# Fewer candidates and four queues: the expert selection of a diffusion backbone on one core

## The chip, the cores and the metric

The kernel runs on one core of a Trainium2 chip. The metric is the device time of one execution in microseconds. The engines are TensorE (PE; its weight loads are PEld), VectorE (DVE), ScalarE (ACT), GpSimd (POOL) and SyncE (SP), which here only issues transfers. TensorE's clock is granted at 2.4 or 1.2 GHz; the profile gives the granted share.

## What is computed

A backbone of two layers over 512 latent tokens and, in layer 0, 256 context tokens. Each layer has a mixer and then a block (PEER) that picks experts for each token. Only that block is touched by the change. Of it, for each block of 128 tokens:

```python
q = (xb @ w_q).reshape(PEER_BLOCK, PEER_HEADS, 2, PEER_DHALF)
s = jnp.einsum('thpd,hpkd->thpk', q, subkeys).astype(jnp.float32)
s1, i1 = lax.top_k(s[:, :, 0], PEER_TOPK)
s2, i2 = lax.top_k(s[:, :, 1], PEER_TOPK)
cand = (s1[..., :, None] + s2[..., None, :]).reshape(PEER_BLOCK, PEER_HEADS, PEER_TOPK * PEER_TOPK)
cidx = (i1[..., :, None] * PEER_NKEYS + i2[..., None, :]).reshape(PEER_BLOCK, PEER_HEADS, PEER_TOPK * PEER_TOPK)
top, pos = lax.top_k(cand, PEER_TOPK)
idx = jnp.take_along_axis(cidx, pos, axis=-1)
g = jax.nn.softmax(top, axis=-1)
ue, ve = u[idx], v[idx]
act = jax.nn.gelu(jnp.einsum('td,thkd->thk', xb, ue).astype(jnp.float32), approximate=False)
return jnp.einsum('thk,thkd->td', (g * act).astype(xb.dtype), ve)
```

There are 8 heads, 128 keys in each half, 16 picks and a model width of 1024; the tables `u` and `v` have 16384 rows in each layer.

## The kernel before

The layers run one after the other: the mixer, then `peer_u`, then `peer_v0` or `peer_v1`. Every fp32 product is made of three matmuls of a high and a low half; ScalarE writes the high half (`uh`, `wqh`, `pqh`, `vh`) and VectorE, sometimes GpSimd, the low half (`ul`, `wql`, `pql`, `vl`) by a subtraction (`split`, L106 and L109).

`peer_u` treats the tiles of 128 tokens in two ways. For the first `ng` tiles (two in layer 0, one in layer 1) it gathers the picked rows of `u` (L899, GpSimd) and takes a dot product with the token on VectorE (L905). For the other `n - ng` tiles (four, three) TensorE multiplies the whole table with the tokens, in 128 steps of 128 table rows (`proj`, L674); ScalarE takes the Gelu (`ga`, L991) and the result goes to DRAM. The gates of these tiles are spread to all 16384 rows by matmuls of one-hot rows (`prep` makes `p1`, `p2e` and `p2` on VectorE, L834 to L837; `gbuild` multiplies, L851, and ScalarE copies to `stg`), and are stored in `gd`. The next stage, `peer_v0` or `peer_v1`, loads them (`gf`) and multiplies them in (L1037).

The first sixteen steps also have a projection each (`q_items`): `project` (the queries of one half of a head), `evac` (`pqh`, `pql`, L717 and L718), `score` (the products with the keys, whose matmuls read `pql`) and `top`, a search of the 16 largest of 128 scores for each tile (`topk16`: five finding instructions, L643 to L647). The weights' low halves `wql` come from GpSimd but for the first two, all `skl` too (`q_load`).

The picks are side work (`stage2`). `cands` adds all 256 pairs of the two lists of 16 for two heads (L766) and searches the 16 largest of 256; `decode` turns a position into the two key numbers by comparing it with 0 to 15 and summing (L789 to L794); `rows` makes the row numbers for the gathers; `soft` is the softmax over a tile's heads (Exp on ScalarE, L802).

What sets the order: at the end of each step a loop takes pieces from three queues (the gathered tiles with their dots in one, the gates of the others, and the modulation products of `mod_items`) by the largest share that is left, until the costs written beside the pieces have used up what the step gives; a piece is held to stand behind `ul` of the next step (`issue_after`). Each engine then works in the order in which its instructions stand. `ul` and `uh` have a raised priority. The searches of the step are issued ahead of this loop:

```python
if 1 <= c <= 2 * PH:
    for f in qi[c - 1][3]:
        f()
```

Of the kernel before, what the change touches and what calls it, by code (L numbers as in the profile page):

```python
# [21 lines left out]
P = 128  # L22
# [3 lines left out]
NLAT = 512  # L26
# [45 lines left out]
def kernel(ctx: ExitStack, tc: tile.TileContext, a: dict, out: bass.AP, dbg=None, stop=None):  # L72
# [13 lines left out]
    tok = [a["tok"][t * P:(t + 1) * P, :] for t in range(NT)]  # L86

# [561 lines left out]
    def peer_u(layer, tiles):  # L649
# [4 lines left out]
        gd = dram.tile([TD // 32, P, P, 32], F32, name=f"gd{layer}")  # L654
# [3 lines left out]
        with ExitStack() as s1:  # L658
# [9 lines left out]
            def proj(ps, wh, wl, blks):  # L668
                for k in range(KD):
                    for x, q in ((wh, 0), (wh, 1), (wl, 0)):  # L670
# [9 lines left out]
                      allow_small_or_imprecise_dtypes=True)  # L680
            urow = [up.tile([P, P], U32, name=f"urow{j}", bufs=1) for j in range(ng)]
# [6 lines left out]
            def q_load(hp):  # L688
# [4 lines left out]
                split(wh, wl, w, eng_lo=vec if hp < 2 else pool)  # L693
# [4 lines left out]
                split(skh, skl, sk, eng_lo=pool)  # L698
# [42 lines left out]
            side, pend, stores = [], [], []  # L741

            def store():
                b, stg, j = stores.pop(0)
                js = slice(j, j + P // GS)
                nc.scalar.dma_start(gd[b][:, js], stg[:, js])
# [5 lines left out]
            def stage2(t):  # L752
                d = {}

                def alloc():
                    d["top"] = up.tile([P, PH, TOPK], F32, name="top", bufs=3)
                    d["pos"] = up.tile([P, PH, TOPK], U32, name="pos", bufs=3)
                    d["if"] = up.tile([P, 16, TOPK], F16, name="if16", bufs=3)
                    d["id"] = [up.tile([P, PH, TOPK], F32, name=f"id{q}", bufs=3) for q in range(2)]

                def cands(h0):
                    def f():
                        vv = v16[t].rearrange("p (h q) k -> p h q k", q=2)
                        c = up.tile([P, 2, TOPK, TOPK], F32, name="cand", bufs=1)
                        hs = slice(h0, h0 + 2)
                        vec.tensor_tensor(c, vv[:, hs, 0, :, None].to_broadcast([P, 2, TOPK, TOPK]),  # L766
                                          vv[:, hs, 1, None, :].to_broadcast([P, 2, TOPK, TOPK]), op=ALU.add)
                        for h in range(2):
                            w_ = up.tile([P, 256], F32, name="candw", bufs=1)
                            topk16(d["top"][:, h0 + h, :], d["pos"][:, h0 + h, :],  # L770
                                   c[:, h].rearrange("p x y -> p (x y)"), w_)
                    return f

                def decode(h0):
                    def f():
                        iv = d["if"].rearrange("p (h q) k -> p h q k", q=2)
                        hs = slice(h0, h0 + 2)
                        qs = slice(2 * h0, 2 * h0 + 4)
                        vec.tensor_copy(d["if"][:, qs], i16[t][:, qs])
                        for q in range(2):  # L780
                            pi = up.tile([P, 2, TOPK], U32, name="pi")
                            if q == 0:
                                vec.tensor_scalar(pi, d["pos"][:, hs], 4, None, op0=ALU.logical_shift_right)
                            else:
                                vec.tensor_scalar(pi, d["pos"][:, hs], 15, None, op0=ALU.bitwise_and)
                            pf = up.tile([P, 2, TOPK], F16, name="pif")
                            vec.tensor_copy(pf, pi)
                            eq = up.tile([P, 2, TOPK, TOPK], F16, name="eq", bufs=1)
                            vec.tensor_tensor(eq, pf[:, :, :, None].to_broadcast([P, 2, TOPK, TOPK]),  # L789
                                              i16v[:, None, None, :].to_broadcast([P, 2, TOPK, TOPK]),  # L790
                                              op=ALU.is_equal)
                            vec.tensor_tensor(eq, eq, iv[:, hs, q, None, :].to_broadcast([P, 2, TOPK, TOPK]),
                                              op=ALU.mult)
                            vec.tensor_reduce(d["id"][q][:, hs], eq, axis=AX.X, op=ALU.add)  # L794
                    return f

                def soft():
                    top = d["top"]
                    g = up.tile([P, PH, TOPK], F32, name="g")
                    sm = up.tile([P, PH], F32, name="gsm")  # L800
                    vec.tensor_tensor(g, top, top[:, :, 0:1].to_broadcast([P, PH, TOPK]), op=ALU.subtract)
                    act.activation(g, g, AF.Exp)  # L802
                    vec.tensor_reduce(sm, g, axis=AX.X, op=ALU.add)
                    vec.reciprocal(sm, sm)
                    vec.tensor_tensor(g, g, sm[:, :, None].to_broadcast([P, PH, TOPK]), op=ALU.mult)
                    d["g"] = g
# [74 lines left out]
                for h0 in range(0, PH, 2):  # L881
                    out_ += [(cands(h0), 4.9), (decode(h0), 3.8)]
# [755 lines left out]
```

## Time and profile before

| | |
|---|---|
| Median of 3 runs | 4072.78 us (4063.73 to 4077.03) |
| The profiled execution | 4070.86 us |
| Its span | 4069.1 us |
| TensorE busy | 3779.4 us, 93% |
| TensorE weight loads | 3221.3 us, 79% |
| VectorE busy | 3287.3 us, 81% |
| ScalarE busy | 1463.4 us, 36% |
| GpSimd busy | 1394.4 us, 34% |
| Transfers | 1036.47 MB, 255 GB/s on average |

Busy times are unions over the whole span; TensorE's matmuls overlap each other, so its share is no measure of distance from its peak. The stages follow each other: layer 0's `peer_u` from 475 to 1632 us, `peer_v0` to 2345, layer 1's mixer to 2726, its `peer_u` to 3516, `peer_v1` to the end.

### The profile page before, as it was taken

To read this page: it belongs to the slowest core of one execution; us is meant where nothing else is said; L and a number is where in the kernel's file an instruction comes from. 1 tells how busy PE (TensorE), PEld (TensorE's weight loads), DVE (VectorE), ACT (ScalarE), POOL (GpSimd) and SP (SyncE) were. 2 spreads that over 40 slices of the span, in tenths; PEclk is the share of its full clock that TensorE was granted. 3 is DMA by queue.
4 is the path that set the end of the run, shared out by engine and by line. 5 is a ranking of instruction groups with operands and counts; after the bars stand their busy time and mean duration, and the time that the engine had idled before them with its cause. 6 is when DMAs were issued, how large, how long until landed. Compare 5 with 4: busy or idle time off the path is not lost. (4 is left out here: it accounts for less than half of the span.)

```text
span 4069.1 us, 53545 instructions
## 1 busy us (share of the span) xinstructions
PE 3779.4 (93%) x19201; PEld 3221.3 (79%) x19201; DVE 3287.3 (81%) x6594; ACT 1463.4 (36%) x2384; POOL 1394.4 (34%) x1010
## 2 busy tenths in 40 slices
PE   6988989999999897999999989888999999899998
PEld 5766777877777675788888789867899999788887
DVE  7776698998999897888888864458898987588887
ACT  4354422233232333322232355542234344333333
POOL 2521225303423244666666412215302222132221
PEclk9999989999999998999999999988999999999999
DMA  7301446548979799999999721046448779799995
GB/s 245 100 3 52 172 141 240 177 167 301 342 261 356 274 368 363 387 390 390 387 391 389 283 84 46 18 172 220 164 159 319 266 268 331 286 385 363 356 356 216
DMA packets 409099, 1036.47 MB, mean 255 GB/s; under 512 B 33024, under 2 KB 167680, under 8 KB 408832
## 3 DMA queue, kind: packets, MB, share of 16 engines
q1 hardware_dynamic: 259360, 498.68, 35.3%
q0 software_dynamic: 114336, 416.34, 27.9%
q10 hardware_dynamic: 35136, 118.05, 7.5%
q8 instruction: 150, 2.46, 0.2%
q14 instruction: 117, 0.96, 0.1%
HBM read 906.05 MB, written 126.88 MB: 254 GB/s over the span
## 5 line engine op out<-in xcount | busy, mean ns | idle before, releaser
L899 POOL DMA_INDIRECT urows<-in_u_rows,urow x384 | 487.5, 1270 | 1124.1 <-DVE urows L905 639.4
L1048 POOL DMA_INDIRECT vrows<-in_v_t,vrow x384 | 594.2, 1547 | 592.5 <-DVE accg L1056 340.1
L674 PE MATMUL aps<-pnh,uh 128*128 128x512 f32 (+1 forms) x2048 | 770.0, 376 | 22.0 <-ACT ga L991 18.4
L674 PE MATMUL aps<-pnh,ul 128*128 128x512 f32 (+1 forms) x2048 | 763.6, 373 | 26.3 <-DVE ul L109 26.0
L674 PE MATMUL aps<-pnl,uh 128*128 128x512 f32 (+1 forms) x2048 | 759.6, 371 | 0.0
L106 ACT CAST uh<-uf 128x1024 fp32r<-128x1024 f32 x256 | 269.2, 1051 | 839.2 <-PE aps L674 815.9
L905 DVE SCALAR_TENSOR_TENSOR urows<-urows,px 128x1024 f32<-128x1024 f32 x384 | 468.7, 1231 | 66.1 <-DMA urows<-in_u_rows,urow 65.4
L106 ACT CAST vh<-vf 128x1024 fp32r<-128x1024 f32 x256 | 269.3, 1053 | 594.5 <-DMA vf<-in_v_t 279.9
L674 PEld LDWEIGHTS aps<-pnh,ul 128*128 128x128 f32 x2048 | 389.8, 190 | 78.7 <-DVE ul L109 34.2
L674 PEld LDWEIGHTS aps<-pnh,uh 128*128 128x128 f32 x2048 | 391.5, 191 | 72.0 <-ACT ga L991 25.4
L109 DVE TENSOR_TENSOR vl<-vf,vh 128x1024 fp32r<-128x1024 f32 x256 | 312.6, 1221 | 166.0 <-ACT vh L106 155.9
L674 PEld LDWEIGHTS aps<-pnl,uh 128*128 128x128 f32 x2048 | 390.5, 191 | 43.2
L109 DVE TENSOR_TENSOR ul<-uf,uh 128x1024 fp32r<-128x1024 f32 x256 | 320.2, 1251 | 79.5 <-ACT uh L106 70.3
L1079 PE MATMUL acc<-vh,vwh 128*128 128x512 f32 x1024 | 317.7, 392 | 23.9 <-ACT vwh L106 23.8
L1079 PE MATMUL acc<-vh,vwl 128*128 128x512 f32 x1024 | 317.3, 391 | 1.3 <-DVE vwl L109 1.1
L1079 PE MATMUL acc<-vl,vwh 128*128 128x512 f32 x1024 | 317.5, 391 | 0.0
L1056 DVE SCALAR_TENSOR_TENSOR vacc<-vrows,gw,vacc 128x1024 f32<-128x1024 f32 x254 | 313.8, 1277 | 0.0
L851 PE MATMUL gps<-p,p 128*128 128x128 f16 x1792 | 243.9, 296 | 14.1 <-DVE p L837 14.1
L1144 PE MATMUL acc<-vh,vwh 128*128 128x512 f32 x768 | 239.3, 393 | 15.2 <-ACT vwh L106 12.1
L1079 PEld LDWEIGHTS acc<-vh,vwh 128*128 128x128 f32 x1024 | 192.8, 189 | 66.2 <-ACT vwh L106 26.4
L851 PEld LDWEIGHTS <-p 128*128 128x128 f16 x1792 | 189.1, 118 | 62.7 <-issue 38.6
L1144 PE MATMUL acc<-vl,vwh 128*128 128x512 f32 x768 | 238.2, 392 | 0.0
(430 smaller groups left out, 7540.8 us busy)
## 6 DMA issues: line engine op xcount, KB each, us to landing
uf<-in_u_t SPq DMA_DIRECT2D x256, 512.0 KB
vf<-in_v_t SPq DMA_DIRECT2D x256, 512.0 KB
gd<-stg ACTq DMA_DIRECT2D x112, 512.0 KB
wmt<-in_w_modT SPq DMA_DIRECT2D x90, 512.0 KB
gad<-ga ACTq DMA_DIRECT2D x64, 512.0 KB
gaf<-gad SPq DMA_DIRECT2D x64, 512.0 KB
gf<-gd SPq DMA_DIRECT2D x32, 1024.0 KB
gad<-ga ACTq DMA_DIRECT2D x64, 384.0 KB
```

The lines of the kernel that those rows point to most:

```text
L106: act.copy(hi, src)
L109: return el.tensor_tensor(lo, src, hi.bitcast(F32), op=ALU.subtract)
L674: pe.matmul(ps[:, o:o + w], x[:, k, :], blk[q][:, k, :w], start=(k == 0 and x is wh and q == 0), stop=(k == KD - 1 and x is wl))
L851: pe.matmul(gp[:, i * P:(i + 1) * P], p1[:, g, :, i], p2[q][:, g, :, i], start=q == 0, stop=q == 1)
L899: nc.gpsimd.indirect_dma_start(out=r, out_offset=None, in_=a["u_rows"], in_offset=bass.IndirectOffsetOnAxis(ap=urow[j][:, k:k + 1], axis=0))
L905: vec.scalar_tensor_tensor(r, r, 1.0, PK["x"][j], op0=ALU.mult, op1=ALU.mult, accum_out=gact[j][:, k:k + 1])
L1048: nc.gpsimd.indirect_dma_start(out=r, out_offset=None, in_=a["v_t"].rearrange("l c k d -> (l c k) d"), in_offset=bass.IndirectOffsetOnAxis ...
L1056: vec.scalar_tensor_tensor(acc, r, gw[:, k:k + 1], acc, op0=ALU.mult, op1=ALU.add)
L1079: pe.matmul(acc[i][hf], x[:, ts_], y[:, hf * 512:(hf + 1) * 512], start=(c == 0 and first), stop=(c == 127 and end))
L1144: pe.matmul(acc[i][hf], x[:, ts_], y[:, hf * 512:(hf + 1) * 512], start=(c == 0 and first), stop=(c == 127 and last))
```

## The change

It changes the side work of `peer_u` and its order.

- `cands` adds only 65 of the 256 pairs: 16 with the largest of the first list, 8 each with the next two, 4 each with the next four, 2 each with the next eight, 1 with the last. It works on two heads at a time for the gathered tiles and on four for the others.
- `decode` finds the first list's place by comparing the position with the 16 starts (`lo16`, not less than) and summing differences of neighbouring key numbers (`prev1`, `dl`); the second's place is the position and a mask that a shift makes.
- The softmax runs per group of two or four heads, behind `decode`, no longer once for a tile.
- `wql` and `skl` are VectorE's in all steps.
- The side work has four queues: routing of the gathered tiles, the gates, the dots, the modulation products. Each has a goal, a first and a last step, and the queue that lies furthest behind its goal is served. A routing piece waits for the step behind its last projection.
- The searches of a step are issued last in it, behind the side work; the pools are exchanged one step later; the gates lie in one DRAM tensor for each tile, and `gf` is loaded in one piece for each.

The core of the diff; in `stage2` only new lines are shown, the old ones stand in the listing above:

```diff
+    gds = [[dram.tile([4, P, P, 32], F32, name=f"gd{v}_{t}") for t in range(n - NG[v])]
+           for v, n in enumerate((NT, NLAT // P))]
...
+            lo16 = up.tile([P, TOPK], F16, name="lo16", bufs=1)
+            for r0, rn, base, step in ((0, 1, 0, 16), (1, 2, 16, 8), (3, 4, 32, 4), (7, 8, 48, 2), (15, 1, 64, 1)):
+                pool.iota(lo16[:, r0:r0 + rn], pattern=[[step, rn]], base=base, channel_multiplier=0,
+                          allow_small_or_imprecise_dtypes=True)
+            c15 = up.tile([P, 4 * TOPK], U32, name="c15", bufs=1)
+            pool.iota(c15, pattern=[[0, 4 * TOPK]], base=15, channel_multiplier=0)
+            prev1 = up.tile([P, 4, TOPK + 1], F16, name="prev1", bufs=1)
+            vec.memset(prev1, 0.0)
...
-                split(wh, wl, w, eng_lo=vec if hp < 2 else pool)
+                split(wh, wl, w)
...
-                split(skh, skl, sk, eng_lo=pool)
+                split(skh, skl, sk)
...
             def stage2(t):
+                H = 2 if t < ng else 4
+                keep = t >= ng
                 d = {}
 
                 def cands(h0):
                     def f():
+                        if h0 == 0:
+                            d["g"] = up.tile([P, PH, TOPK], F32, name="g" if keep else f"g{t}", bufs=2 if keep else 1)
+                            if keep:
+                                d["id"] = up.tile([P, 2, PH, TOPK], F32, name="idk")
+                        hs = slice(h0, h0 + H)
+                        top = d["top"] = up.tile([P, H, TOPK], F32, name="top")
+                        pos = d["pos"] = up.tile([P, H, TOPK], U32, name="pos")
+                        vv = v16[t].rearrange("p (h q) k -> p h q k", q=2)[:, hs]
+                        c = up.tile([P, H, 65], F32, name="cand", bufs=1)
+                        for o, r0, rn, m in ((0, 0, 1, 16), (16, 1, 2, 8), (32, 3, 4, 4), (48, 7, 8, 2), (64, 15, 1, 1)):
+                            vec.tensor_tensor(c[:, :, o:o + rn * m].rearrange("p h (r m) -> p h r m", m=m),
+                                              vv[:, :, 0, r0:r0 + rn, None].to_broadcast([P, H, rn, m]),
+                                              vv[:, :, 1, None, 0:m].to_broadcast([P, H, rn, m]), op=ALU.add)
+                        for h in range(H):
+                            w_ = up.tile([P, 65], F32, name="candw", bufs=1)
+                            topk16(top[:, h, :], pos[:, h, :], c[:, h, :], w_)
                     return f
 
                 def decode(h0):
                     def f():
+                        iv = i16[t].rearrange("p (h q) k -> p h q k", q=2)[:, h0:h0 + H]
+                        pos = d["pos"]
+                        dl = up.tile([P, 2, H, TOPK], F16, name="dl", bufs=1)
+                        vec.tensor_copy(prev1[:, :H, 1:], iv[:, :, 0, :])
+                        vec.tensor_copy(dl[:, 1], iv[:, :, 1, :])
+                        vec.tensor_tensor(dl[:, 0], prev1[:, :H, 1:], prev1[:, :H, :TOPK], op=ALU.subtract)
+                        pq = up.tile([P, 2, H, TOPK], F16, name="pq", bufs=1)
+                        vec.tensor_copy(pq[:, 0], pos)
+                        ps_ = pos.rearrange("p h k -> p (h k)")
+                        pt = up.tile([P, H * TOPK], U32, name="pt", bufs=1)
+                        vec.tensor_scalar(pt, ps_, 4, None, op0=ALU.logical_shift_right)
+                        vec.tensor_tensor(pt, c15[:, :H * TOPK], pt, op=ALU.logical_shift_right)
+                        vec.tensor_tensor(pt, ps_, pt, op=ALU.bitwise_and)
+                        vec.tensor_copy(pq[:, 1], pt.rearrange("p (h k) -> p h k", k=TOPK))
+                        if not keep:
+                            d["t"] = up.tile([P, 2, H, TOPK], F32, name="idt")
+                        dst = d["id"][:, :, h0:h0 + H] if keep else d["t"]
+                        for q, (tab, op) in enumerate(((lo16, ALU.is_ge), (i16v, ALU.is_equal))):
+                            eq = up.tile([P, H, TOPK, TOPK], F16, name="eq", bufs=1)
+                            vec.tensor_tensor(eq, pq[:, q, :, :, None].to_broadcast([P, H, TOPK, TOPK]),
+                                              tab[:, None, None, :].to_broadcast([P, H, TOPK, TOPK]), op=op)
+                            vec.tensor_tensor(eq, eq, dl[:, q, :, None, :].to_broadcast([P, H, TOPK, TOPK]),
                                               op=ALU.mult)
+                            vec.tensor_reduce(dst[:, q], eq, axis=AX.X, op=ALU.add)
                     return f
 
+                def soft(h0):
+                    def f():
+                        top = d["top"]
+                        g = d["g"][:, h0:h0 + H]
+                        sm = up.tile([P, H], F32, name="gsm")
+                        vec.tensor_tensor(g, top, top[:, :, 0:1].to_broadcast([P, H, TOPK]), op=ALU.subtract)
+                        act.activation(g, g, AF.Exp)
+                        vec.tensor_reduce(sm, g, axis=AX.X, op=ALU.add)
+                        vec.reciprocal(sm, sm)
+                        vec.tensor_tensor(g, g, sm[:, :, None].to_broadcast([P, H, TOPK]), op=ALU.mult)
+                    return f
+
...
+                def heads(h0):
+                    need = 2 * (h0 + H) + 1
+                    last = None if keep else rows(h0)
+                    return [(cands(h0), 1.6 * H, need), (decode(h0), 0.7 + 1.4 * H, need), (soft(h0), 1.0, need)] + \
+                        ([(last, 0.5, need)] if last else [])
+
+                build = [(prep(t0), gbuild(t0, 0), gbuild(t0, 1)) for t0 in range(0, P, 8)] if keep else []
+                return heads, tr, fin, build, weigh
...
+            st2 = [stage2(t) for t in range(n)]
+            route = []
+            for h0 in range(0, PH, 2):
+                route += [x for t in range(ng) for x in st2[t][0](h0)] + [(found, 0.0, 0)]
+            heads = [[x for h0 in (0, 4) for x in st2[t][0](h0)] + [(st2[t][1], 0.0, 0)] for t in range(ng, n)]
+            one = heads[0]
+            for t in range(ng, n):
+                nxt = heads[t + 1 - ng] if t + 1 < n else []
+                one.append((st2[t][2], 1.0, 0))
+                for pf, g0, g1 in st2[t][3]:
+                    one.append((pf, 2.75, 2 * PH + 1))
                     for gf in (g0, g1):
                         pend.append(gf)
                         if len(pend) > 3:
+                            one.append((pend.pop(0), 0.0, 0))
                         if nxt:
+                            one.append(nxt.pop(0))
+                one += nxt
+            one += [(f, 0.0, 0) for f in pend] + [(flush, 0.0, 0)]
+            total_dots = P * ng
+            dots = [(dot(x), 1.3, (x, 1)) for x in range(total_dots)] + [(st2[t][4], 0.3, (total_dots - 1, 1)) for t in range(ng)]
+            bgq = [(f, 1.33 * (2 if layer == 0 and x < 24 else 1), 0) for x, f in enumerate(bg)]
+            queues = [route, one, dots, bgq]
+            goal = [(4, 18), (8, 118), (8, 125), (17, 124)]
+            whole = [sum(x[1] for x in q) for q in queues]
+            left = list(whole)
             slack = []
             for c in range(128):
+                pe_us = TD * 24 / 2260 + (TT * 30 / 2200 if c < 2 * PH else 0.4)
+                slack.append(pe_us - 1.3 - (1.45 * n + 1.2 if 1 <= c <= 2 * PH else 0.0) if c < SIDE_END else 0.0)
             given, total = 0.0, sum(whole)
             spent = 0.0
+            reach = [sum(slack[:c]) / sum(slack) for c in range(129)]
+
+            def lag(q, c):
+                c0, c1 = goal[q]
+                want = min(max((reach[c] - reach[c0]) / (reach[c1] - reach[c0]), 0.0), 1.0)
+                return want * whole[q] - (whole[q] - left[q])
+
+            def can(q, c):
+                if not queues[q]:
+                    return False
+                need = queues[q][0][2]
+                return need[0] < at["rows"] if isinstance(need, tuple) else need <= c or c == 127
+
...
-                if 1 <= c <= 2 * PH:
-                    for f in qi[c - 1][3]:
-                        f()
-                if c == 2 * PH:
+                if c == 2 * PH + 1:
...
-                    ok = [q for q in range(3) if queues[q] and (queues[q][0][2] <= c or c == 127)]
+                    ok = [q for q in range(len(queues)) if can(q, c)]
                     if not ok or (spent > given and c < 127):
                         break
-                    q = max(ok, key=lambda q: left[q] / whole[q])
+                    q = max(ok, key=lambda q: lag(q, c))
                     f, w, _ = queues[q].pop(0)
                     with tc.issue_after(los[min(c + LAG, 127)]):
                         f()
                     left[q] -= w
                     spent += w
+                if 1 <= c <= 2 * PH:
+                    for f in qi[c - 1][3]:
+                        f()
...
-            nc.sync.dma_start(st["gf"], gd[:, :, c:c + 4, :].rearrange("b p j t -> p b j t"))
+            for t, x in enumerate(gd):
+                nc.sync.dma_start(st["gf"][:, 4 * t:4 * t + 4], x[:, :, c:c + 4, :].rearrange("b p j t -> p b j t"))
```

The order of three places, where line numbers of the changed program are its own. The first is VectorE in a projection step of layer 0, up to the low half `pql` that TensorE's scores wait for. Before, the ninth of them (`urows` are dots, `tkw` and `i16` belong to the searches of the scores):

```order
L905 SCALAR_TENSOR_TENSOR urows_5859,gact0_4267<-urows_5859,px0_3513 128x1024
L646 MAX v16_5_4253<-tkw_5838 128x8
L905 SCALAR_TENSOR_TENSOR urows_6019,gact1_4268<-urows_6019,px1_3514 128x1024
L647 MAX_INDEX i16_5_4259<-v16_5_4253,tkw_5838 128x8
L905 SCALAR_TENSOR_TENSOR urows_6022,gact0_4267<-urows_6022,px0_3513 128x1024
L905 SCALAR_TENSOR_TENSOR urows_6025,gact1_4268<-urows_6025,px1_3514 128x1024
L718 TENSOR_TENSOR pql_5863<-aps_5759,pqh_5862 128x768
L109 TENSOR_TENSOR ul_6042<-uf_5695,uh_6041 128x1024
```

In the change, the same projection (`idt`, `pq` and `pt` belong to a routing group's `decode`):

```order
L808 TENSOR_TENSOR eq_6045<-pq_6037,lo16_4271 128x512
L800 TENSOR_TENSOR pt_6039<-c15_4277,pt_6039 128x32
L810 TENSOR_TENSOR eq_6045<-eq_6045,dl_6033 128x512
L801 TENSOR_TENSOR pt_6039<-pos_6014,pt_6039 128x32
L812 TENSOR_REDUCE idt_6044<-eq_6045 128x32
L111 TENSOR_TENSOR wql_5955<-wq_5952,wqh_5954 128x1024
L728 TENSOR_TENSOR pql_5893<-aps_5792,pqh_5892 128x768
L802 CAST pq_6037<-pt_6039 128x32
```

The dots ahead of `pql` are gone; a routing group and `wql` stand there. The second place is VectorE behind the last `ul` of layer 0. Before:

```order
L109 TENSOR_TENSOR ul_14210<-uf_14149,uh_14209 128x1024
L835 TENSOR_TENSOR p2e_13853<-iota_7170,idT_12903 128x1024
L905 SCALAR_TENSOR_TENSOR urows_13784,gact0_4267<-urows_13784,px0_3513 128x1024
L837 TENSOR_TENSOR p20_13851<-p2e_13853,idT_12903 128x1024
L837 TENSOR_TENSOR p21_13852<-p2e_13853,idT_12903 128x1024
L905 SCALAR_TENSOR_TENSOR urows_13787,gact1_4268<-urows_13787,px1_3514 128x1024
L834 TENSOR_TENSOR p1_13885<-iota_7170,idT_12903 128x1024
```

In the change:

```order
L111 TENSOR_TENSOR ul_14244<-uf_14183,uh_14243 128x1024
L923 SCALAR_TENSOR_TENSOR urows_13857,gact0_4283<-urows_13857,px0_3520 128x1024
L154 SCALAR_TENSOR_TENSOR wmt_13905,mcol_96<-wmt_13905,crow_4291 128x1024
L923 SCALAR_TENSOR_TENSOR urows_13860,gact1_4284<-urows_13860,px1_3521 128x1024
L857 TENSOR_TENSOR p1_13932<-iota_7374,idT_12768 128x1024
L858 TENSOR_TENSOR p2e_13935<-iota_7374,idT_12768 128x1024
L923 SCALAR_TENSOR_TENSOR urows_13899,gact0_4283<-urows_13899,px0_3520 128x1024
L860 TENSOR_TENSOR p20_13933<-p2e_13935,idT_12768 128x1024
L860 TENSOR_TENSOR p21_13934<-p2e_13935,idT_12768 128x1024
L923 SCALAR_TENSOR_TENSOR urows_13902,gact1_4284<-urows_13902,px1_3521 128x1024
```

The four one-hot rows here are the change's last ones, and behind them 14 dots in all (with those above) and 6 modulation products are left; before, 15 one-hot rows (with those above), 8 dots and 2 modulation products stand behind this `ul`. The third place is ScalarE in a projection step of layer 0, where before no Exp stands. In the change:

```order
L741 COPY sc_5165<-tp_5166 128x512
L821 ACT_TABLE_LOAD
L821 ACTIVATE g0_5249<-g0_5249 128x32
L741 COPY sc_5165<-tp_5180 128x256
L108 CAST skh_5196<-sk_5194 128x128
L108 CAST wqh_5388<-wq_5386 128x1024
L727 CAST pqh_5326<-aps_5200 128x768
L108 CAST uh_5540<-uf_5136 128x1024
L1022 ACT_TABLE_LOAD
L1022 ACTIVATE ga_5361<-aps_5336 128x512
```

An Exp (`g0`) with its table load has come between the copies of the scores, and the next Gelu (`ga`) loads its table again. In all, ScalarE's order has 79 table loads in the change and 44 before.

## Rows read from the trace of the kernel before

**Rows 1.** Stretches: us, busy time (instructions) of each engine, granted clock, DMA share, GB/s.

```profile
475.00:784.00 309.00, 282.46 (x1455) 242.48 (x1455) 272.20 (x994) 75.24 (x115) 124.63 (x89) 0.93 0.60 203
784.00:1577.00 793.00, 742.25 (x3578) 585.16 (x3577) 728.14 (x1544) 249.49 (x354) 240.65 (x190) 0.98 0.80 293
1577.00:1632.00 55.00, 27.32 (x151) 21.15 (x151) 35.97 (x66) 13.38 (x23) 21.37 (x19) 0.76 0.96 358
1632.00:2345.00 713.00, 704.76 (x3080) 580.28 (x3080) 628.25 (x687) 215.71 (x274) 444.20 (x256) 0.99 1.01 373
...
2726.00:2940.00 214.00, 190.61 (x980) 172.22 (x978) 170.42 (x648) 61.28 (x97) 100.34 (x71) 0.93 0.59 198
2940.00:3516.00 576.00, 568.34 (x3455) 555.40 (x3454) 482.03 (x950) 222.79 (x333) 106.72 (x92) 0.99 0.73 259
```

**Rows 2.** Waits of TensorE, 784 to 1577 us: total us, times, longest.

```profile
PE aps L674 <- DVE ul L109: 21.3, 9, 6.2
PE aps L674 <- ACT ga L991: 17.4, 17, 1.4
```

**Rows 3.** Waits of TensorE, 475 to 784 us.

```profile
PE tp L114 <- DVE pql L718: 24.4, 9, 5.5
```

**Rows 4.** Waits of TensorE, 2726 to 2940 us.

```profile
PE tp L114 <- DVE pql L718: 22.2, 6, 14.5
```

**Rows 5.** Timeline of ScalarE: start us, duration us, instruction.

```profile
768.02 0.59 ACT L991 ACTIVATE ga<-aps 128x512 f32<-128x512 f32 x1
784.08 0.59 ACT L991 ACTIVATE ga<-aps 128x512 f32<-128x512 f32 x1
791.68 0.59 ACT L991 ACTIVATE ga<-aps 128x512 f32<-128x512 f32 x1
797.28 0.59 ACT L991 ACTIVATE ga<-aps 128x512 f32<-128x512 f32 x1
...
842.11 0.58 ACT L991 ACTIVATE ga<-aps 128x512 f32<-128x512 f32 x1
...
848.65 0.59 ACT L991 ACTIVATE ga<-aps 128x512 f32<-128x512 f32 x1
```

**Rows 6.** Groups by shape: total us, mean ns of one, idle before and its cause.

```profile
L905 DVE SCALAR_TENSOR_TENSOR urows<-urows,px 128x1024 f32<-128x1024 f32 x384 | 468.7, 1231 | 66.1 <-DMA urows<-in_u_rows,urow 65.4
...
L644 DVE FIND_INDEX8 i<-v,sc 128x8 uint32<-128x128 f32 x160 | 45.3, 283 | 0.0
...
L644 DVE FIND_INDEX8 pos<-top,cand 128x8 uint32<-128x256 f32 x80 | 33.3, 417 | 0.0
...
L766 DVE TENSOR_TENSOR cand<-v 128x512 f32<-128x512 f32 x40 | 27.6, 689 | 0.0
...
L785 DVE TENSOR_SCALAR pi<-pos 128x32 uint32<-128x32 uint32 x40 | 6.9, 171 | 0.0
...
L109 DVE TENSOR_TENSOR wql<-wq,wqh 128x1024 fp32r<-128x1024 f32 x4 | 4.9, 1226 | 5.9 <-ACT wqh L106 5.9
...
L109 POOL TENSOR_TENSOR wql<-wq,wqh 128x1024 fp32r<-128x1024 f32 x28 | 68.5, 2448 | 69.1 <-ACT wqh L106 68.9
```

**Rows 7.** Waits of VectorE, 475 to 784 us.

```profile
DVE urows L905 <- DMA urows<-in_u_rows,urow: 9.9, 5, 3.5
```

**Rows 8.** Waits of VectorE, 784 to 1577 us.

```profile
DVE urows L905 <- DMA urows<-in_u_rows,urow: 47.6, 34, 4.0
```

**Rows 9.** Timelines of VectorE and of TensorE at the end of layer 0's `peer_u`.

```profile
1587.56 1.22 DVE L109 TENSOR_TENSOR ul<-uf,uh 128x1024 fp32r<-128x1024 f32 x1 [0.64 <-ACT uh L106]
...
1631.85 1.22 PE L1079 MATMUL acc<-vh,vwh 128*128 128x512 f32 x2 [19.93 <-ACT vwh L106]
```

**Rows 10.** Timeline of ScalarE round the first softmax of layer 0.

```profile
828.11 0.31 ACT L802 ACTIVATE g<-g 128x128 f32<-128x128 f32 x1 [6.28 <-DVE g L801]
...
829.37 1.28 ACT L991 ACT_TABLE_LOAD   x1
830.66 0.60 ACT L991 ACTIVATE ga<-aps 128x512 f32<-128x512 f32 x1
```

More of the change, by code (lines that the diff above doesn't have):

```diff
@@ L653, in peer_u @@
         TD = TT - ng * P
-        gd = dram.tile([TD // 32, P, P, 32], F32, name=f"gd{layer}")
+        gd = gds[layer]
         gad = dram.tile([64, P, 2, TD], F32, name=f"gad{layer}")
@@ L752, in stage2 @@
             def stage2(t):
+                H = 2 if t < ng else 4
+                keep = t >= ng
                 d = {}
[L755 to L759, printed above, removed]
                 def cands(h0):
@@ L775, in f @@
                     def f():
[L776 to L792, printed above, removed]
@@ L808, in tr, with ids @@
+                def ids(h0):
+                    ks = slice(h0 * TOPK, (h0 + H) * TOPK)
+                    return ks, [d["t"][:, q].rearrange("p h k -> p (h k)") for q in range(2)]
                 def tr():
                     tp = pp.tile([P, 512], F32, name="tp", bufs=2)
-                    for q, x in enumerate((d["id"][0], d["id"][1], d["g"])):
+                    for q, x in enumerate((d["id"][:, 0], d["id"][:, 1], d["g"])):
                         pe.transpose(tp[:, q * P:(q + 1) * P], x.rearrange("p h k -> p (h k)"), ident)
@@ L854, in f @@
                         if o == 28:
-                            stores.extend((((t - ng) * P + t1) // 32, d["stg"], j) for j in range(0, P, P // GS))
+                            stores.extend((t - ng, t1 // 32, d["stg"], j) for j in range(0, P, P // GS))
                         elif stores and o % 8 == 0:
@@ L927, in peer_u @@
             qi = [q_items(hp) for hp in range(2 * PH)]
-            heads, fins, gbs = zip(*[stage2(t) for t in range(ng, n)])
-            early = []
-            routes = [stage2(t) for t in range(ng)]
-            for p in range(PH // 2):
-                for r, _, _ in routes:
-                    early += [(f, w, 4 * p + 4) for f, w in filter(None, r[p])]
-                early.append((found, 0.0, 0))
-                early += [(dot(x), 1.3, 0) for x in range(2 * TOPK * ng * p, 2 * TOPK * ng * (p + 1))]
-            early += [(s_[0], s_[1], 2 * PH) for _, s_, _ in routes] + [(w[0], w[1], 2 * PH) for _, _, w in routes]
-            side += heads[0]
-            for t in range(n - ng):
-                nxt = list(heads[t + 1]) if t + 1 < n - ng else []
-                side.append((fins[t], 1.0))
-                for pf, g0, g1 in gbs[t]:
-                    side.append((pf, 2.75))
+            st2 = [stage2(t) for t in range(n)]
[9 more added lines that the diff above has]
+                    one.append((pf, 2.75, 2 * PH + 1))
                     for gf in (g0, g1):
```

52 lines of the change are left out of this document (5 added, 47 removed).

## The prediction

> **What bounds the kernel now.** I read the stages first [rows 1]. Layer 0's table stage is 475 to 1632 us and layer 1's 2726 to 3516; no other stage's code changes, apart from one load that is cut into pieces. In 784 to 1577, the steps of layer 0 that have no projection, TensorE is busy 742 of 793 us and VectorE 728: neither has room, and each waits for the other in turn. TensorE's waits there end with VectorE's low half of a table block (`ul`, 21.3 us) and with ScalarE's Gelu output behind it (17.4 us) [rows 2]. In the projection steps, 475 to 784, TensorE waits 24.4 us for VectorE's low half of the projection (`pql`) [rows 3], and its granted clock is 0.93 of 2.4 GHz [rows 1], the mean of stretches at that level and at 1.2 GHz. Layer 1 shows the same wait, 22.2 us [rows 4], and after it almost none: VectorE is busy 482 of 576 us there [rows 1].
>
> How short a step can be is read from the times at which ScalarE begins the Gelu output of consecutive steps [rows 5]: 16.07 us with a projection, 5.60 us without, 6.54 us with one group of eight gate matmuls, so 0.94 us a group. From 784 to 1577 there are 108 steps and, by the order of TensorE, 118 such groups: 605 + 111 = 716 us. Of 793 us, 77 can be won at most. The sixteen projection steps (485 to 784) have a floor of 257 us in 299: 42 us.
>
> **What the change does to VectorE's work.** *Searches.* A finding instruction takes 417 ns over 256 elements and 283 over 128 [rows 6], 1.05 ns per element; 191 elements fewer are 0.20 us, and a search has five such instructions: 1.0 us. There are 48 searches in layer 0 (six tiles, eight heads) and 32 in layer 1: 48 and 32 us less. No row is shorter than 128 elements; if 65 cost what 128 do, it is 32 and 21 us. *Candidate sums.* 24 sums of 0.689 us [rows 6] (16.5 us) become 16 groups of five small ones, each at most the 0.171 us of a 32-element row [rows 6]: 13.7 us, a gain of 3; in layer 1 about 2. *Decoding.* The large comparisons cover the same elements in fewer instructions, and eight small helpers a group replace five in each of more groups: I take 2 and 1 us less. *Softmax* runs per group: 64 small instructions instead of 24 in layer 0, 40 instead of 16 in layer 1, 5 and 3 us more. *Splits of the projection weights* come from GpSimd: 14 of 1.226 us and 16 of about 0.28 us [rows 6] in each layer, 22 us more. GpSimd loses 28 of 2.448 us in all [rows 6], which costs nothing, and its gathers no longer stand behind them.
> Net: layer 0 -48-3-2+5+22 = -26 us, layer 1 -32-2-1+3+22 = -10.
>
> **Where it falls.** In layer 0 the order takes 46 of 54 dot products with gathered rows out of the projection steps (57 us at the 1.231 of their row [rows 6]) and puts about six more routing groups in (some 40 us), four modulation products (5) and the splits (22): VectorE gets some 8 us more there, the later steps 34 less.
>
> *Projection steps of layer 0.* If VectorE's 8 us pass on one for one, it is +8 or, with the clock, up to +15; if the evener order removes what is lost, -42. For a gain: VectorE's 9.9 us of waits for gathers [rows 7] go with the dots; the first excerpt of the order shows `pql` free of them. Against: VectorE's own sum in steps 2 to 6 is over 18 us against TensorE's 16.07. I take 0.
> *Later steps of layer 0.* VectorE is the later one, so its 34 us come off one for one, as long as 77 are not reached: -34, bounds 0 and -77.
> *The handover to the next stage.* The last `ul` begins at 1587.6, the first matmul of the next stage at 1631.9 [rows 9]: 44.3 us, in which the last one-hot rows (`p`), their gate matmuls, the stores and a load of what was stored follow each other. The order now has the last `p` eight places behind that `ul` instead of twenty-eight; twenty places of some 0.7 us are 14 us by which the stores leave earlier. But 14 dots and 6 modulation products are left on VectorE: 20 x 1.23 + 4 x 0.68 = 27 us, then 2.5 us to the first matmul, plus the `ul` itself (1.2): 31 us. Twenty transfers of 0.5 MB, six of them ahead of time, with 2 MB of stores and 2.5 MB of loads, are 11.9 MB; at the 373 GB/s of the next stage [rows 1] that is 32 us. So some 33 instead of 44: -10, bounds 0 and -14.
> *Layer 1.* In the projection steps 18 instead of 23 dots lie in the three steps round the long wait; VectorE has 44 us of room in 214 for the 22 us of splits [rows 1]: -3. Later there are only 5 us of waits to win: -5. Together -8, bounds +15 and -28.
> *The gate load* in four pieces (three in layer 1) adds issues on SP, whose transfers run well ahead: 0. *Softmax on ScalarE*: 26 instead of 10, each with a load of the Exp table and one of the Gelu table back, 1.28 us each [rows 10]; the order shows 79 table loads instead of 44. 35 x 1.28 = 45 us on an engine that is busy 338 of 1157 us in layer 0's stage (first three lines) and 284 of 790 in layer 1's [rows 1]; a `ga` may be a step late, so I take 0. If that cover is gone, it is the third rival.
>
> Of these loads the Trainium skill ("ScalarE: Activation LUTs", What ACT_TABLE_LOAD costs and the section on table sets) says that one takes 1283 ns and is followed by a drain, 2.66 us in all, and that calls should be batched by set, which speaks against this change. The trace agrees with the 1283 and not with the drain: the Gelu starts at 830.66, 1.29 us after its load began at 829.37 [rows 10]. By the page the 35 loads would be 93 us of ScalarE instead of 45.
>
> Sum: 0 - 34 - 10 - 8 = -52 us. The profiled execution took 4070.86 us (its span 4069.1 and 1.8 around it), 1.9 under the median of the runs: 4070.9 - 52 = **4019 us**.
>
> **Rivals.**
> 1. *All waits go.* With VectorE under TensorE in each step, TensorE reaches its floors: -77 later, -30 of 42 in the projections, -11 at the handover, -25 in layer 1: 4071 - 143 = 3928. For: both engines' busy times are near the span, so small excesses make most waits. Against: VectorE would still have 694 of 716 us.
> 2. *The transfers take VectorE's place.* 46 dots of 0.5 MB (24 MB) move into the later steps, which moved 293 GB/s x 793 us = 232 MB [rows 1]; 256 MB at 373 GB/s are 686 us, under the floor, but a dot waits for its own gather, 47.6 us of such waits lay here [rows 8], and the list is only four rows deep. If each dot waits as much as now and the shorter steps double it, the 34 us are lost: 4071 - 18 = 4053.
> 3. *ScalarE's queue holds back `uh` (slower).* Exp stands in the queue of the casts `uh` that `ul` and the matmuls need. One of ten Exp waited 6.28 us for VectorE's subtraction with the queue behind it [rows 10]. If each of the 16 additional ones does, 101 us: 4019 + 101 = 4120. It decides from 52/16 = 3.3 us each. Against: the other nine waited little, and the subtraction stands early in its step by the order.
> 4. *`pql` comes later still.* The splits stand ahead of `pql`, as the excerpt shows. In these steps 24.4 us of waits went with 42 us lost, 1.7 for each. 22 us so passed on are 37 in layer 0 (4056), and as much in layer 1 if its room is in the wrong steps (4093).
> That the searches do not shrink below their 128-element time is a bound of the first term (16 us less in layer 0): 4035.
>
> **How the numbers follow.** 0.3%, about what a measurement of this kernel can tell from no change, is 12 us: faster is under 4060.6, slower over 4085. The forecast has a chance of 0.52 (its own range 3985 to 4045), rival 1 0.12, rival 2 0.16, rival 3 0.10, rival 4 0.10. Faster: 0.52 + 0.12 + 0.13 + 0.01 = 0.78; slower: 0.09 + 0.03 = 0.12; the rest, 0.10, within. The range holds the forecast, rival 2, the lower part of rival 4 and the near part of rival 1: 3955 to 4070.
>
> **What would show it.** Right: MAX8 and FIND_INDEX8 over 65 elements near 0.21 us; VectorE busy about 1010 us in layer 0's stage instead of 1036 (the first three lines of [rows 1]); TensorE's wait for `ul` in the later steps well under 21 us, and these steps some 34 us shorter; a gap of some 20 us at the handover that a dot ends and not the gate load; 26 Exp with two loads each and hardly a wait of TensorE behind them. Wrong: waits of TensorE for `pql` over 24 us in layer 0 with a granted clock under 0.93 (rival 4); waits of dots for gathers over 80 us (rival 2); ScalarE idle for VectorE's subtraction over 50 us (rival 3); later steps near 716 us (rival 1).

## The result, and the profile after

The changed kernel takes 4016.77 us (median of 4 runs, 4014.09 to 4019.17) against 4071.81: a ratio of 0.9866 [0.9848, 0.9884]. The forecast was 4019. The profiled execution took 4018.06 us, its span 4015.8.

Both spans are cut at the same events: the start of the first and of the 17th Gelu output of a layer, of layer 0's last `ul`, of the first matmul of the next stage, and in layer 1 of the last Gelu output. All lengths of stages below are cut so.

| Stage, us | Before | After | Difference | Forecast |
|---|---|---|---|---|
| Projection steps, layer 0 | 299.1 | 286.9 | -12 | 0 |
| Later steps, layer 0 | 803.5 | 765.4 | -38 | -34 |
| Handover | 44.3 | 55.9 | +12 | -10 |
| Next stage and layer 1's mixer | 1101.7 | 1105.9 | +4 | 0 |
| Projection steps, layer 1 | 206.5 | 201.1 | -5 | -8 with the next |
| Later steps, layer 1 | 576.5 | 563.8 | -13 | |

The fourth line lies between 1098.6 and 1105.9 in all but one of the kernels run, though most do the same there, so 4 us say nothing. The sum was met, but three of its terms were not: 22 us too good at the handover, 22 too bad in layer 0's projection steps and in layer 1. That these cancel is luck. The stretches after, as in [rows 1]:

```profile
485.60:772.50 286.90, 266.73 (x1419) 228.97 (x1418) 262.62 (x1180) 84.14 (x126) 15.71 (x13) 0.95 0.39 126
772.50:1538.00 765.50, 745.50 (x3669) 592.05 (x3669) 697.18 (x1453) 273.20 (x382) 309.60 (x234) 0.99 0.91 333
1538.00:1594.00 56.00, 12.35 (x61) 9.63 (x60) 29.71 (x52) 5.30 (x10) 23.44 (x20) 0.65 1.00 374
1594.00:2307.00 713.00, 702.85 (x3080) 580.01 (x3080) 627.04 (x683) 214.34 (x273) 449.88 (x255) 0.99 1.01 372
2699.00:2901.00 202.00, 182.30 (x953) 164.78 (x951) 171.36 (x744) 64.70 (x101) 30.29 (x27) 0.95 0.50 171
2901.00:3465.00 564.00, 562.84 (x3452) 551.97 (x3450) 454.04 (x907) 235.04 (x346) 126.80 (x104) 1.00 0.80 279
```

The first two lines of the kernel before, with the same cut:

```profile
485.00:784.00 299.00, 272.57 (x1419) 234.45 (x1417) 267.62 (x990) 67.46 (x107) 123.34 (x88) 0.93 0.59 199
784.00:1588.00 804.00, 751.61 (x3625) 592.38 (x3625) 738.50 (x1559) 252.13 (x357) 246.63 (x194) 0.98 0.80 292
```

VectorE works 41 us less in layer 0's later steps, and they are 38 shorter: nearly one for one, as forecast. Two of its groups by shape, which answer to [rows 6]:

```profile
L646 DVE FIND_INDEX8 pos<-top,cand 128x8 uint32<-128x65 f32 x80 | 17.7, 221 | 0.0
...
L779 DVE TENSOR_TENSOR cand<-v 128x64 f32<-128x64 f32 x56 | 9.2, 216 | 0.0
```

A finding instruction takes 221 ns over 65 elements instead of 417 over 256: 0.98 us a search, as forecast. The waits after, of TensorE and VectorE in layer 0's later steps, then of TensorE in layer 0's and in layer 1's projection steps, as in [rows 2 to 4] and [rows 8]:

```profile
PE aps L676 <- ACT ga L1022: 6.6, 5, 1.9
...
PE aps L676 <- DVE ul L111: 2.9, 4, 1.0
```

```profile
DVE urows L923 <- DMA urows<-in_u_rows,urow: 28.9, 24, 3.2
```

```profile
PE tp L116 <- DVE pql L728: 17.1, 9, 5.2
```

```profile
PE tp L116 <- DVE pql L728: 18.5, 6, 11.0
```

TensorE's wait for `ul` is nearly gone (2.9 of 21.3 us), those for `pql` are not (17.1 of 24.4, 18.5 of 22.2).

### The profile page after: what moved, and what is told of

Read it like the earlier page. It is cut to its first block, busy times and chain, and to the rows that moved or that the text cites. A ratio compares the mean times of both kernels' runs of the same rounds, so it can differ in the third digit from the quotient of the medians.

```text
span 4015.8 us, 54004 instructions
## 1 busy us (share of the span) xinstructions
PE 3754.6 (93%) x19201; PEld 3208.5 (80%) x19201; DVE 3220.2 (80%) x6734; ACT 1512.0 (38%) x2435; POOL 1317.5 (33%) x962
## 5 line engine op out<-in xcount | busy, mean ns | idle before, releaser
L1111 PE MATMUL acc<-vh,vwh 128*128 128x512 f32 x1024 | 317.7, 392 | 48.4 <-ACT vwh L108 48.3
L1176 PE MATMUL acc<-vh,vwh 128*128 128x512 f32 x768 | 238.4, 392 | 13.5 <-ACT vwh L108 12.9
L108 ACT CAST vwh<-gaf 128x512 fp32r<-128x512 f32 (+1 forms) x256 | 144.3, 564 | 277.5 <-DVE gaf L1069 178.5
```

Source lines behind the costliest of these rows:

```text
L108: act.copy(hi, src)
L1111: pe.matmul(acc[i][hf], x[:, ts_], y[:, hf * 512:(hf + 1) * 512], start=(c == 0 and first), stop=(c == 127 and end))
L1176: pe.matmul(acc[i][hf], x[:, ts_], y[:, hf * 512:(hf + 1) * 512], start=(c == 0 and first), stop=(c == 127 and last))
```

## The experiments

**The two halves apart.** The first kernel is the kernel before with the new picks alone, the second the changed kernel with the old ones:

```diff
 picks_alone: cands() and decode() of the kernel before
-c = up.tile([P, 2, TOPK, TOPK], F32, name="cand", bufs=1)
+c = up.tile([P, 2, 65], F32, name="cand", bufs=1)
...
-for q in range(2):
+for q, (tab, op) in enumerate(((lo16, ALU.is_ge), (i16v, ALU.is_equal))):
...
-(cands(h0), 4.9), (decode(h0), 3.8)
+(cands(h0), 3.2), (decode(h0), 3.5)
 order_alone: the same two of the changed kernel, the other way
-(cands(h0), 1.6 * H, need), (decode(h0), 0.7 + 1.4 * H, need)
+(cands(h0), 2.45 * H, need), (decode(h0), 1.9 * H, need)
...
```

> The kernel before with 65 candidate sums and the new decode (two heads at a time), but its own three queues, its softmax once for a tile, GpSimd's splits and its searches ahead of the side work. Theory of less work (VectorE's removed work is the gain): in layer 0's steps without a projection VectorE spends some 60 us less on candidates, so these steps lose 35 to 50 of their 77 us above the floor, layer 1 some 5 to 10: 4010 to 4035 us. Rival (the order is the gain): the work removed fills up with waits of dots for gathers, which stay at 48 us or rise: 4055 to 4072.

> The changed kernel with 256 candidate sums and the old comparisons (two heads at a time), all else as in the change: queues, goals, searches last, splits on VectorE, softmax per group. Theory of less work: layer 0's later steps go back to some 800 us, the projection steps get longer by part of the 20 us of splits: 4065 to 4095. Rival (the order is the gain): 4020 to 4040.

4032.11 us, 0.9898 [0.9883, 0.9913], and 4052.68 us, 0.9945 [0.9931, 0.9959]. Layer 0's later steps in the one and in the other (the columns of [rows 1]):

```profile
785.70:1559.00 773.30, 744.36 (x3632) 594.09 (x3632) 703.87 (x1722) 250.85 (x357) 262.92 (x193) 0.99 0.84 306
```

```profile
771.50:1572.00 800.50, 755.85 (x3666) 600.16 (x3666) 743.69 (x1501) 272.95 (x381) 284.14 (x236) 0.97 0.89 319
```

The picks alone take 30.5 us off these steps, the order alone 3, both 38: they are the work's gain. The projection steps are the order's: 299.9 us with the picks alone, 284.2 with the order alone (before 299.1). So is the loss at the handover: 42.2 and 54.6 (44.3). Layer 1's later steps lose 9 us by the picks alone, 11 by the order alone and 13 by both. So each theory was right in one stage, and neither for the whole: the first time lies in its theory's range, the second between its two ranges.

**Splits, searches, softmax.** Three parts of the change undone one at a time:

```diff
 splits_pool
-split(wh, wl, w)
+split(wh, wl, w, eng_lo=vec if hp < 2 else pool)
-split(skh, skl, sk)
+split(skh, skl, sk, eng_lo=pool)
 search_first: peer_u(), ahead of the swap and the side work
+if 1 <= c <= 2 * PH:
+    for f in qi[c - 1][3]:
+        f()
 if c == 2 * PH + 1:
     swap()
...
-if 1 <= c <= 2 * PH:
-    for f in qi[c - 1][3]:
-        f()
 soft_tile: heads(), and soft() over all eight heads
-(soft(h0), 1.0, need)]
+([(soft(h0), 1.0, need)] if h0 + H == PH else [])
```

> The changed kernel with the low halves of the projection weights and keys on GpSimd again, as before. Theory of less work: 22 us leave VectorE in each layer's projection steps, where TensorE waits 17 to 20 us for pql, so 5 to 15 us are won: 4002 to 4012. Rival (GpSimd's split of 2.4 us is late, and the gathers stand behind it): no gain or up to 15 us slower, 4015 to 4032.

> The changed kernel with the searches of a projection step issued ahead of the side work again. Theory of less work: VectorE's sum in a step is the same and pql stands behind both, so 4010 to 4025. Rival (searches last bring routing and dots forward, and with them pql and the gathers): projection steps some 10 to 20 us longer, 4027 to 4037.

> The changed kernel with one softmax for each tile behind its last decode, as before: 10 Exp instead of 26, and fewer loads of activation tables. Forecast's view (ScalarE has room, table loads are hidden): no change, 4012 to 4021. Third rival (each Exp and its loads hold back uh or the scores' copies by 0.5 us or more): 8 us or more faster, below 4009.

*Splits:* 4022.33 us, 0.9883 [0.9866, 0.9899]. Not faster, and the projection steps are longer, 292.9 and 205.9 us (286.9 and 201.1 before the edit; 287.2 to 288.5 and 200.2 to 200.4 in the two kernels below, `gf_front` and `few_rows`, that leave these steps alone). Some 21 us of splits have left VectorE in layer 0 (14 of 1.22 us, 15 of 0.28), and yet it is as busy there (261.5 us, 262.6 before the edit). Its timeline shows why, with GpSimd's beside it:

```profile
595.05 2.28 DVE L824 TENSOR_TENSOR g<-g,gsm 128x32 f32<-128x32 f32 x1
...
699.67 2.43 DVE L802 CAST pq<-pt 128x64 f16<-128x64 uint32 x1
```

```profile
594.87 2.40 POOL L111 TENSOR_TENSOR wql<-wq,wqh 128x1024 fp32r<-128x1024 f32 x1 [6.89 <-ACT wqh L108]
...
698.78 3.27 POOL L111 TENSOR_TENSOR wql<-wq,wqh 128x1024 fp32r<-128x1024 f32 x1 [6.53 <-ACT wqh L108]
```

A product of 32 elements, 188 ns in the changed kernel, takes 2.28 us and ends within 0.1 us of GpSimd's split, and so does a cast (195 ns otherwise). In all, ten VectorE instructions in layer 0's projection steps are over 0.3 us longer than their like in the changed kernel, together 16.3 us, and each runs beside such a split. The Trainium skill ("SBUF — State Buffer", Who interferes with whom) says that the two engines share a pair of ports as an exclusive lock held for a whole instruction, which a VectorE operation with two inputs and a cast can need; both rows agree.

*Searches:* 4021.39 us, 0.9872 [0.9857, 0.9887], projection steps 288.3 us: no difference that can be measured, as the theory of less work had it.

*Softmax:* 4014.35 us, 0.9859 [0.9839, 0.9879], no change. Of ScalarE's table loads, the Exp's groups in the changed kernel and here:

```profile
L821 ACT ACT_TABLE_LOAD x26 | 33.4, 1283 | 1.6 <-ACT ga L1022 1.2
```

```profile
L823 ACT ACT_TABLE_LOAD x9 | 11.5, 1283 | 1.6 <-ACT ga L1025 1.5
```

Seventeen loads of 1283 ns less, and as many back to the Gelu's table, are worth nothing that can be measured: the third rival falls.

**The handover.** VectorE's, then SyncE's timeline of the changed kernel behind layer 0's last `ul`:

```profile
1537.86 1.23 DVE L111 TENSOR_TENSOR ul<-uf,uh 128x1024 fp32r<-128x1024 f32 x1 [1.66 <-ACT uh L108]
...
1557.22 1.23 DVE L154 SCALAR_TENSOR_TENSOR wmt<-wmt,crow 128x1024 f32<-128x1024 f32 x1 [4.27 <-DMA wmt<-in_w_modT]
...
1575.21 1.22 DVE L923 SCALAR_TENSOR_TENSOR urows<-urows,px 128x1024 f32<-128x1024 f32 x1
...
1592.35 0.69 DVE L1069 TENSOR_TENSOR gaf<-gaf,gf 128x512 f32<-128x512 f32 x1 [12.91 <-DMA gf<-gd]
```

```profile
1577.18 6.02 SPq L1062 DMA_DIRECT2D gf<-gd  x4
```

The last dot ends 39 us behind the start of that `ul`, where 28 were reckoned, since VectorE waited 7.1 us for gathers and 4.3 for a load; only then the gate load is issued, and VectorE waits 12.9 us for it. The trace does not show what released that load. The guess is that `gf` lies on addresses that `gact` had, which the last products read, so the next kernel lays it out elsewhere. The others end the side work earlier, or take away five of the next stage's gathers:

```diff
 gf_front: v_chunk()
+if c % 4 == 0 and layer == 0:
+    st["gf"] = vr.tile([P, TT // 32, 4, 32], F32, name="gf", bufs=rb[2])
 vf = vr.tile([P, D], F32, name="vf", bufs=rb[0])
 end120: peer_u()
-if c < SIDE_END else 0.0)
+if c < (120 if layer == 0 else SIDE_END) else 0.0)
 few_rows
-VB0 = 8
+VB0 = 3
```

> The changed kernel, with the buffers of layer 0's gate loads (gf) laid out first in the next stage's pool, so that they no longer share addresses with gact, which the last products behind the dots read. Theory (the gate load is issued only when that memory is free, 0.4 us after the last dot's product): it is issued some 20 us earlier, and the first matmul of the next stage follows the last dot by some 4 us instead of 17: 12 to 14 us less, 4002 to 4008. Rival (the load is late because gathers and loads fill the transfers): it lands at the same time, 4013 to 4021.

> The changed kernel, whose side work in layer 0 is to be given out by step 120 instead of 124, so that by the order no dot stands behind the last ul (14 before). Theory (the handover is made of late dots, and VectorE stood idle in part of the last steps): handover 25 to 30 us instead of 56, the later steps 10 to 18 longer: 4000 to 4012. Rival (VectorE is full, what is moved forward lengthens the steps by as much): 4013 to 4022.

> The changed kernel with three buffers instead of eight for the gathered rows of layer 0's next stage, so that five gathers of 0.5 MB (2.5 MB) no longer go ahead of the gate load. Theory (the handover is bound by the transfers, which are full at 380 to 420 GB/s in it): the handover is some 6 us shorter, 49 to 51 us instead of 56, whatever the next stage loses by the shorter list. Rival (the late dots and the order of VectorE alone make it): 54 to 58 us. Total between 4005 and 4030.

*gf_front:* 4016.28 us, 0.9868 [0.9847, 0.9889], handover 55.9: no change, the rival. In it the Gelu output's load waits until 1574.41. The gate load behind it is issued 34.3 us behind the last `ul` instead of 39.3, ahead of the last dot (1577.78), so it no longer waits for the products; yet VectorE's product with it starts 54.5 us behind that `ul` in both kernels:

```profile
1574.41 0.33 SPq L1060 DMA_DIRECT2D gaf<-gad  x1
1574.84 7.64 SPq L1065 DMA_DIRECT2D gf<-gd  x4
```

*few_rows:* the handover is 48.3 us, 7.6 shorter for 2.5 MB less; the next stage with the mixer takes 1308.1 instead of 1105.9, since three rows are too short a list for it (VectorE waits 275.6 us for them), and the total is far outside the range expected (4216.19 us, 1.0362 [1.034, 1.0384]). The gate load is issued at the same place, 39.5 us behind the last `ul`, and VectorE waits 5.1 us for it instead of 12.9. So transfers bound the handover. Two stretches of the changed kernel's, and one line of its transfers from 1545 to 1600:

```profile
1556.00:1566.00 10.00, 0.00 (x0) 0.00 (x0) 5.61 (x9) 0.00 (x0) 2.36 (x3) 0.50 1.03 419
1566.00:1577.00 11.00, 0.00 (x0) 0.00 (x0) 6.86 (x16) 0.62 (x2) 8.86 (x9) 0.50 1.03 417
```

```profile
DMA packets 9061, 20.66 MB, mean 376 GB/s; under 512 B 690, under 2 KB 4499, under 8 KB 9057
```

*end120:* 4011.81 us, 0.9856 [0.9835, 0.9876], which the intervals do not tell from the changed kernel. The handover falls to 33.0, but the later steps take 14 us more and the projection steps 6:

```profile
778.00:1557.00 779.00, 750.99 (x3683) 595.67 (x3682) 717.26 (x1489) 275.19 (x383) 332.88 (x243) 0.99 0.92 338
```

VectorE's 20 us that came from behind the last `ul` (697.2 to 717.3 busy) make 14 of length.

**Bursts, and beyond the change.** Of layer 1's 18.5 us of waits for `pql`, 14.3 lie in two steps. VectorE's dots in them (us, busy time and instructions, granted clock, DMA share, GB/s):

```profile
2763.10:2804.60 41.50, 21.63 (x36) 0.79 0.92 334
```

Eighteen dots (two instructions each) in 41.5 us, with a granted clock of 0.79 of 2.4 GHz: shares that nothing could use in the first steps are carried over and spent at once when the first rows are found. The next kernel does not carry them:

```diff
 even: peer_u()
-given += slack[c] * total / sum(slack)
+rest = sum(slack[c:])
+given = min(given, spent) + (slack[c] * sum(left) / rest if rest else 0.0)
 even_end120: with the edit of end120 too
 even_deep5: even, and
-UB0 = 4
+UB0 = 5
-d["t"] = up.tile([P, 2, H, TOPK], F32, name="idt")
+d["t"] = up.tile([P, 2, H, TOPK], F32, name="idt", bufs=1)
 even_bg: even, and bgq
-else 1), 0) for x, f in enumerate(bg)]
+else 1), 2 * PH + 1) for x, f in enumerate(bg)]
```

> The changed kernel, where a step's unspent share of side work is not carried over but spread over all steps that follow. Theory (the long wait for pql in layer 1, 11.5 us, and those of layer 0 come from bursts, ten dots in one step, that carried shares let out): layer 1's projection steps 8 to 14 us shorter, layer 0's 0 to 8: 3996 to 4010. Rival (they come from VectorE's fixed work and the order of evac): 4013 to 4021.

> The version without carried shares, and layer 0's side work given out by step 120. Theory (two separate places, so the gains add): the 20 us of layer 1's projection steps and 5 us of the earlier end, 3988 to 3996. Rival (the earlier end crowds layer 0's steps, whose VectorE has no room): 3996 to 4006.

> The version without carried shares, with five buffers instead of four for the gathered rows of the dots in layer 0 (idt has one buffer instead of two, to make room). Theory (dots wait 29 us for gathers in layer 0's later steps; the list is too short): that wait falls by half, and the later steps by 5 to 12 us: 3985 to 3993. Rival (transfers are the limit there, 0.91 of their time in use, or the waits lie beside TensorE's own work): 3994 to 4001.

> The version without carried shares, with the modulation products of layer 0 served only from step 17 on. Theory (in the projection steps VectorE's sum is the limit; steps 3 and 5, where these products stand, are 22.7 and 23.3 us long against 16.1): projection steps 10 to 15 us shorter, later steps 15 to 25 longer, in all 3997 to 4010. Rival (the waits for pql there come from the order alone): projection steps within 5 us, total 4012 or more.

*even:* 3997.18 us, 0.9822 [0.9805, 0.9838]. Layer 1's projection steps take 179.9 us instead of 201.1, at a granted clock of 1.00, with this wait left; its later steps take 5 back:

```profile
2696.00:2876.00 180.00, 175.41 (x952) 159.87 (x951) 152.69 (x717) 63.37 (x98) 11.03 (x10) 1.00 0.42 141
```

```profile
PE tp L116 <- DVE pql L728: 4.6, 5, 1.7
```

That is more than the 8 to 14 us of the theory. Layer 0's projection steps stay at 287.4: what this edit takes away costs nothing there.

*even_end120:* 3994.27 us, 0.9811 [0.9794, 0.9828], in the theory's range, but the intervals do not tell it from `even`. The stages bear out the rival: 24 us less at the handover, 21 more ahead of it.

*even_deep5:* 3983.06 us, 0.9785 [0.9769, 0.9801], the fastest. The wait for gathers falls from 27.8 us to 3.7 and the later steps from 760.3 to 749.6. Later steps of layer 0 and VectorE's wait in them:

```profile
778.00:1528.00 750.00, 740.71 (x3661) 591.60 (x3660) 694.56 (x1453) 269.96 (x378) 308.11 (x233) 0.99 0.92 339
```

```profile
DVE urows L923 <- DMA urows<-in_u_rows,urow: 3.7, 2, 2.6
```

*even_bg:* 4018.77 us, 0.9871 [0.9852, 0.989]. Without modulation products VectorE is busy 35 us less in layer 0's projection steps, which take 269.3 us instead of 287.4; the later steps take 36 more (795.9), not 15 to 25.

```profile
486.80:756.00 269.20, 258.42 (x1418) 221.80 (x1417) 227.59 (x1113) 83.74 (x126) 21.07 (x17) 0.99 0.32 110
```

So VectorE's sum bounds those steps too, at half a microsecond for one; in the later steps 34 us more of VectorE's work make these 36. Half of the 18 us is TensorE's own time (258.4 us busy instead of 266.9, at a granted clock of 0.99 instead of 0.95).

## Why the prediction was right, and where it was not

*Later steps, -34 (-38): right, and shown.* In the six kernels whose stretch stands above their length is VectorE's busy time and 55 to 69 us. The picks alone give 30.5 for 34.6 of VectorE's time.

*VectorE's work, -26 and -10 (-42 and -25 over the stages): mis-sized.* Counted in the traces, each VectorE instruction from the end of the one before it, the searches came as reckoned (45.5 and 30.0 us less for 48 and 32), and so did the splits in themselves (18.9 and 19.3 more for 22). Sums (5.7 and 4.3 less), softmax (2.6 and 1.9 more) and decoding (0.7 and 5.5 less) are a few us off. The step that failed is that GpSimd's loss of the splits "costs nothing", and so "22 us more" as their net price: on GpSimd they hold up VectorE's own instructions. In the kernel before, ten VectorE instructions of layer 0's stage and five of layer 1's are over 0.3 us longer than the median of their like, together 11.9 and 7.0 us. Each runs beside a GpSimd split, and the changed kernel has none. Five of the ten are `ul`, 1.22 us otherwise; one of them, and the split beside it:

```profile
696.54 2.50 DVE L109 TENSOR_TENSOR ul<-uf,uh 128x1024 fp32r<-128x1024 f32 x1
```

```profile
695.41 2.54 POOL L109 TENSOR_TENSOR wql<-wq,wqh 128x1024 fp32r<-128x1024 f32 x1
```

Moved back, the splits leave VectorE's busy time as it was in layer 0's projection steps, and 8 us lower in layer 1's (162.9 of 171.4).

*Projection steps of layer 0, 0 (-12): inside its bounds, too low.* The step that failed is "VectorE gets some 8 us more there" (its own terms add up to 10): VectorE is busy 5 us less, 262.6 instead of 267.6; the 11.9 us of hold-up above, all of it in these steps, are most of the difference. The order gives the gain (284.2 us with the order alone), and the splits are some 6 us of it; the place of the searches is none. Of the 12 us, 7 are shorter waits for `pql` and 6 TensorE's own time (266.7 us busy instead of 272.6, at a granted clock of 0.95 instead of 0.93). What the departure of the dots and what the queues give was not tried apart.

*Handover, -10 (+12): wrong in sign.* The step that failed is "11.9 MB", 32 us at 373 GB/s. In 56 us at 374 GB/s 20.9 MB moved: gathers and loads of the next stage, which go ahead of the gate load, were left out of the count. The prediction's own row for 1577 to 1632 us (358 GB/s, 55 us) already holds 19.7 MB. So the dots waited for gathers, and not a dot but the gate load ended the gap. The stores did leave 14 us earlier, as reckoned (11.0 us behind the last `ul` instead of 25.0), but that was worth nothing, since what the load waited for was not the stores alone.

*Layer 1, -8 (-18): too low.* Either half alone takes 9 to 11 us off the later steps, for which 5 were allowed; why the halves do not add was not tried. The burst in the projection steps stayed: 18 dots in two steps were seen as fewer than before, not as the cause of the wait that they are.

*ScalarE, 0: right.* Softmax once for a tile changes nothing that can be measured; the 1283 ns of a table load, and no more, is also what the trace after shows: in 64 of 79 cases ScalarE's next operation starts within 1.30 us of the load's start. *The gate load, 0:* its pieces were not tried alone; the next stage's 4 us lie within the scatter.

*Rivals.* All waits go: later steps 765, not near 716. Transfers take VectorE's place: not as foretold, for the dots' waits fell from 47.6 us to 28.9; but a fifth buffer takes 11 us more off the steps. ScalarE's queue: its waits for VectorE's subtraction rose from 10.9 us to 34.0 in the two stages, under the 50 set, and fell to 7.8 with the softmax once for a tile, without a change of the time; refuted. `pql` later still: not seen (17.1 us instead of 24.4).

## What to carry to other kernels

Where an engine in order is full, less work on it is worth nearly its busy time (38 of 41 us and 31 of 35 here), and moved work comes back (14 us for 20 in one kernel, 36 for 34 in another): price both by that engine's busy time in that stage. Work saved on VectorE by a GpSimd split may be no saving: look for VectorE instructions that take far longer than their like and end with, or soon after, a GpSimd instruction. A planner that carries unused shares over lets out bursts; drop them. Count all megabytes queued ahead of a load, not those of the change alone.

## What was not expected of the hardware

A VectorE product of 32 elements took 2.28 us beside a GpSimd split of 2.40, and 0.19 otherwise; a table block's `ul` took 2.50 us beside one, and 1.22 otherwise. With one core at work the transfers reached 419 GB/s over 10 us; the Trainium skill ("DMA: Bandwidth & Descriptors", Measured) gives 425 for one core at 16 MB, and the trace agrees. One more gather buffer of 0.5 MB took the dots' waits from 27.8 us to 3.7, although the transfers were already in use 0.91 of the time.
